# Interleaving a head's gate projection with the next head's query projection

## The chip, the cores and the metric

The kernel runs on one core of a Trainium2 chip. The metric is the device time of one execution in microseconds. A core has a matrix engine (PE, with its weight loads listed as PEld), a vector engine (DVE), an activation engine (ACT), a general engine (POOL) and a queue engine that starts transfers (SP). Each engine works through its own list of instructions in order, and waits on semaphores for the others.

## What is computed

Two layers over 1024 latent tokens of width 1024, with 256 context tokens. The first layer is attention with 16 query heads and 4 key/value heads of width 128, the second a convolution module. The time here is about the first layer; its heads are, cut to what matters:

```python
proj = h_lat @ w_in
q = apply_rope(split_heads(proj[..., :q_end], N_Q_HEADS), cos, sin)
k = apply_rope(split_heads(proj[..., q_end:k_end], N_KV_HEADS), cos, sin)
v = split_heads(proj[..., k_end:v_end], N_KV_HEADS)
z = proj[..., v_end:]
...
o = windowed_attention(q, k, v, kc, vc, sink)
y = (o * jax.nn.silu(z)) @ w_out
```

A query sees the latent keys within 128 positions of it and all context keys. `z` is the gate: one column block of 128 for each head, as for `q`.

## The kernel before

All data are fp32. Each product is made of three matmuls on fp32r parts (high by high, high by low, low by high), so a weight chunk of 1024 x 128 is loaded (`wraw`), copied to its high part on ACT (`whi`) and reduced to its low part on POOL (`wlo`) before PE can use it. `WStream` does this in the order of a list of chunks: z of head n, q of head n + 1, and after every fourth head k and v of the next group.

In the attention stage each head has 8 steps, one for each block of 128 queries. A step issues, in this order on PE: the scores of the next block (`scores`, 6 matmuls into a `pss` bank), a share of projection work (`fill`, usually 12 matmuls into a `psg` bank), from time to time the product with the values (`pv`, into `pso`), and the transposes of the current block's probabilities (`transposes`, into the other kind of `pss` bank). Between scores and transposes DVE takes the maximum with the mask, ACT the exponential, and POOL divides by the sum (`p_page`). After the transposes ACT copies the high part (`pthi`) and DVE the low part (`ptlo`); until both are done the bank can't take the scores of the step after next.

`fill` draws matmuls from a queue of generators, 24 matmuls for each half of 512 tokens. When a half is done, `finish` issues its evaluation: for z a tanh on ACT (`zs_page<-psg`) and a product on DVE; for q and k the rotation (`rope`): a copy on ACT, two transfers that swap the halves of the partitions, a product with the cosine on DVE, a product with the sine and a sum on POOL, a high copy on ACT and a low part on POOL (`ql_page` or `kl_page`). It takes three of six small buffers (`half`).

Two other streams run beside this. `low_parts` splits the output weights: each step it may load a page (`low_page`), take a high copy on ACT (`lhi_half`), subtract on POOL, or write the result back (`wolA`, `wolC`). `ada_rest` multiplies modulation weights on DVE (`mask_page<-dww_raw` or `wsum_raw`).

After heads 3, 7 and 11 the loop regroups: it runs the k and v projections of the next group with no steps between. Between heads, the next head's queries must be enqueued ahead of its first scores:

```python
        if nxt and nxt[1] == 0:
            fill(1000, ("q", h + 1))
        if nxt and not regroup:
            scores(*nxt)
```

PE keeps the order of the program text. On DVE, ACT, POOL and SP a scheduler decides the order when the program is built. Pages of 4 KB per partition come from a first-in first-out list (`Pages`), so the order of frees decides which tile a load must wait for. All instructions are recorded at line 89, in a helper, so groups are told apart by tile names.

Of the kernel before, what the change touches and what calls it, by code (L numbers as in the profile page):

```python
# [19 lines left out]
NH = 16  # L20
# [74 lines left out]
def backbone_kernel(  # L95
# [23 lines left out]
    def nm(s):  # L119
        uid[0] += 1  # L120
        return f"{s}_{uid[0]}"
# [12 lines left out]
    def ps_g():  # L134
        return ps.tile([P, 512], F32, tag="g", name=nm("psg"), bufs=2)
# [13 lines left out]
    def act(out, in_, func, **kw):  # L149
        return A.activation(out=out, in_=in_, func=func, **kw)  # L150
# [4 lines left out]
    def stt(out, in0, scalar, in1, op0, op1):  # L155
        return V.scalar_tensor_tensor(out=out, in0=in0, scalar=scalar, in1=in1, op0=op0, op1=op1)

    def split_lo(eng, lo, full, hi):
        return tt(eng, lo, full, hi.bitcast(F32), ALU.subtract)
# [99 lines left out]
    cidx = {}  # L259
# [14 lines left out]
    wsA = WStream(chunks, nraw=4, lo_eng=lambda i: V if i < 4 else G)  # L274
# [545 lines left out]
    def gemm_half(wc, half, o):  # L820
        wh, wl = wc
        sl = slice(half * 512, half * 512 + 512)
        for kt in range(KT):
            PE.matmul(o, wh[:, kt], Hh[kt][:, sl], start=kt == 0, stop=False)
            yield
            PE.matmul(o, wh[:, kt], Hl[kt][:, sl], start=False, stop=False)
            yield
            PE.matmul(o, wl[:, kt], Hh[kt][:, sl], start=False, stop=kt == KT - 1)
            yield
# [38 lines left out]
    def finish(kind, n, half, o, d, ropes=None, hold=None):  # L868

        sl = slice(half * 512, half * 512 + 512)  # L870
        if kind in "kv" and half == 2:
            c = kvt[n][2]
            if kind == "k":
                act(c[:, 0], o[:, 0:CT], AF.Copy)
                i = split_lo(V, c[:, 1], o[:, 0:CT], c[:, 0])
                while hold:
                    hold.pop()(i)
                return None
        if kind in "qk":
            return rope(o, sl, d[0][:, sl], d[1][:, sl], ropes, hold)  # L880
        if kind == "z":
            act(d[:, sl], o, AF.Tanh, scale=0.5)
            stt(d[:, sl], d[:, sl], 1.0, o, ALU.add, ALU.mult)
            return None
        w = CT if half == 2 else 512
        f = hp.alloc(F32, None, "vf")
        act(f[:, 0:w], o[:, 0:w], AF.Copy)

        def tail():
            if half == 2:  # L890
                vt_split(f, CT, *(c[:, i].rearrange("p (a b) -> p a b", b=P) for i in (2, 3)))
            else:
                vt_split(f, 512, *(t[:, half * 4:half * 4 + 4] for t in d))
            hp.free(f)

        return tail

    def target(kind, n):

        if kind == "q":  # L900
            qt[n] = d = (pg.alloc(F32R, [1024], "qh"), pg.alloc(F32R, [1024], "ql"))
        elif kind == "k":
            kvt[n] = [pg.alloc(F32R, [1024], "kh"), pg.alloc(F32R, [1024], "kl"), pg.alloc(F32R, [4, CT], "kvc")]
            d = kvt[n][0:2]
        elif kind == "v":
            kvt[n] += [pg.alloc(F32R, [TB, P], "vh"), pg.alloc(F32R, [TB, P], "vl")]
            d = kvt[n][3:5]
        else:
            zt[n] = d = pg.alloc(F32, [1024], "zs")
        return d  # L910
# [10 lines left out]
    def job(key):  # L921
        kind, n = key
        i = cidx[key]
        wc = wsA.need(i)
        d = target(kind, n)
        wsA.load()
        late = None
        hold = [] if kind == "k" else None
        for half in PARTS[kind]:
            o = ps_g()  # L930
            gh = gemm_ctx(wc, o) if half == 2 else gemm_half(wc, half, o)
            for m, _ in enumerate(gh):
                yield
                if m == DEFER - 1 and late:
                    late()
            if half == PARTS[kind][0] and wsA.ns <= i + 1:
                wsA.split()
                wsA.load()
            late = finish(kind, n, half, o, d, hold=hold)
        if late:  # L940
            vlate[n] = late
        wsA.done(i)
        if key == ("v", NG - 1):
            for t in Hc:
                pg.free(*t)

    def run(gen):
        for _ in gen:
            pass

    fillq = deque()
    finished = set()

    def fill(n, until=None):
        while n > 0 and fillq and until not in finished:
            try:
                next(fillq[0][1])
                n -= 1
            except StopIteration:
                finished.add(fillq.popleft()[0])  # L960

    def enqueue(key):
        fillq.append((key, job(key)))

    ptile = {}

# [55 lines left out]
    def pv(h, half):  # L1022
        g = h // 4
        c, vh, vl = kvt[g][2:5]
        o = ps_o()
        q0 = half * 4
        work = [(*(c[:, n, i * P:i * P + P] for n in (2, 3)), slice(13 + 4 * i, 17 + 4 * i), slice(0, 512)) for i in range(2)]
        for kb in range(max(q0 - 1, 0), min(q0 + 4, TB - 1) + 1):
            qa, qz = max(kb - 1, q0), min(kb + 1, q0 + 3)
            b0 = 1 + 4 * (1 - (kb - qa)) + (qa - q0)  # L1030
            n = qz - qa + 1
            if n == 1 and kb > qa:
                work.append((vh[:, kb], vl[:, kb], slice(0, 5, 4), slice(256, 512)))
            elif n == 1:
                work.append((vh[:, kb], vl[:, kb], slice(9, 22, 12), slice(0, 256)))
            else:
                work.append((vh[:, kb], vl[:, kb], slice(b0, b0 + 5 * (n - 1) + 1, 5),
                             slice((qa - q0) * P, (qz - q0 + 1) * P)))
        for n, (a, b, ps_, os_) in enumerate(work):
            last = n == len(work) - 1  # L1040
            PE.matmul(o[:, os_], a, pthi[:, ps_], start=n == 0, stop=False)
            PE.matmul(o[:, os_], a, ptlo[:, ps_], start=False, stop=False)
            PE.matmul(o[:, os_], b, pthi[:, ps_], start=False, stop=last)
        sl = slice(half * 512, half * 512 + 512)
        oz = hp.alloc(F32, None, "oz")
        stt(oz[:, 0:512], o, 0.5, zt[h][:, sl], ALU.mult, ALU.mult)
        SY.dma_start(out=ozd[h, :, sl], in_=oz[:, 0:512])
        hp.free(oz)
        if half:
            pg.free(zt.pop(h))  # L1050
            pg.free(*qt.pop(h))
# [49 lines left out]
    lows = low_parts()  # L1101
    lstate = ["shut"]
    pvq = deque()
    enqueue(("z", 0))
    enqueue(("q", 1))
    fill(18)
    while tails:
        tails.pop()()
# [2 lines left out]
    for i, (h, qb) in enumerate(steps):  # L1111
        if qb == 0:
            for n in (() if h % 4 == 3 else (h + 1,) if h % 4 or not h else (h, h + 1)):
                enqueue(("z", n))
                if n + 1 < NH:
                    enqueue(("q", n + 1))
        if (h, qb) == (NH - 1, EARLY_FROM - 2):
            run(lows)
        if h == NH - 1 and EARLY_FROM - 2 <= qb < EARLY_FROM:
            next(projA)  # L1120
        if (h, qb) == (NH - 1, EARLY_FROM):
            next(projA)
            fillq.append((("wo", 0), early_proj()))
        if lstate[0] == "open" or h and (h % 4 < 3 or qb < LOWS):
            lstate[0] = next(lows, "shut")
        nxt = steps[i + 1] if i + 1 < len(steps) else None
        regroup = nxt and nxt[1] == 0 and nxt[0] % 4 == 0
        if nxt and nxt[1] == 0:
            fill(1000, ("q", h + 1))
        if nxt and not regroup:  # L1130
            scores(*nxt)
        if not regroup:
            fill(15 if h and h % 4 == 0 and qb < 4 else FILL)
        if pvq:
            pv(*pvq.popleft())
        if regroup:
            g = nxt[0] // 4
            old = kvt[g - 1]
            run(job(("k", g)))
            transposes(h, qb)  # L1140
            run(job(("v", g)))
            pv(h, 1)
            pg.free(*old)
            scores(*nxt)
            vlate.pop(g)()
            continue
        transposes(h, qb)
        if qb % 4 == 3:
            pvq.append((h, qb // 4))
        for _ in range(2 if qb == 1 or qb == 6 and h % 2 else 1):  # L1150
            next(adag, None)
# [72 lines left out]
    dq, pq = deque(), deque()  # L1224
# [502 lines left out]
```

## Time and profile before

| what | value |
| --- | --- |
| median of 3 runs | 1756.32 us (1753.38 to 1756.82) |
| the profiled execution, its time | 1754.72 us |
| its span, first to last instruction | 1752.9 us |
| mean granted TensorE clock | 0.996 |
| PE busy | 1720.7 us, 98% of the span |
| attention stage, about 100 to 860 us | PE busy 753.28 of 760 us |

A row names an engine, an operation, and the tiles that it writes and reads. A wait in brackets is the time that the engine stood idle ahead of the instruction, and what ended it. In the chain of work that ended last, "issue" is time in which nothing in the profile was waited for.

### The profile page before, as it was taken

The numbers are of one execution on the slowest core, as the hardware profiler recorded it, in microseconds if no ns is written. First come the engines' busy times: TensorE is split into PE (matmuls) and PEld (weight loads), VectorE is DVE, ScalarE is ACT, GpSimd is POOL, SyncE is SP. The second block draws the span as 40 slices with busy tenths as digits, with TensorE's granted clock in tenths as the row PEclk, the third lists the DMA queues.
The fourth block names the chain that finished last, engine by engine and source line by source line (L and its number), as shares of the span: only waits on it lengthen the run. The fifth ranks groups of instructions, "written<-read, shape, count | busy, mean of one in ns | idle before, by whom it ended". The sixth has DMA issues, their size and how long they took to land.

```text
span 1752.9 us, 23877 instructions
## 1 busy us (share of the span) xinstructions
PE 1720.7 (98%) x8420; PEld 1424.8 (81%) x8420; DVE 1148.3 (66%) x2079; ACT 889.4 (51%) x1548; POOL 895.4 (51%) x705
## 2 busy tenths in 40 slices
PE   7999999999999999999999999999999999999997
PEld 4788888888888888888888888888888888788886
DVE  6755564556546563656315189999999999867823
ACT  7555553445345444545334355554665564466731
POOL 0245654566636565653101267998898888130300
PEclk9999999999999999999999999999999999999999
DMA  9334443444334542436777733011121202377971
GB/s 313 107 82 139 136 133 85 145 147 145 100 105 143 152 142 87 136 119 203 279 250 239 241 90 105 13 54 31 43 79 36 91 30 79 120 254 243 325 264 48
DMA packets 195324, 242.45 MB, mean 138 GB/s; under 512 B 11798, under 2 KB 126790, under 8 KB 195204
## 3 DMA queue, kind: packets, MB, share of 16 engines
q1 hardware_dynamic: 188516, 230.10, 40.3%
q10 hardware_dynamic: 6688, 10.83, 2.6%
q8 instruction: 66, 1.08, 0.3%
q14 instruction: 54, 0.44, 0.1%
HBM read 188.70 MB, written 41.69 MB: 131 GB/s over the span
## 4 chain that ended last, share of the span: by engine, by line
PE 86%; DMA 5%; DVE 3%; POOL 2%; ACT 2%; issue 2%; SPq 1%; ACTq 0%; POOLq 0%; DVEq 0%
PE psg L89 44%; PE pss L89 22%; PE pso L89 19%; DMA araw_page<-in_ada_w_dram 1%; POOL rope_half L89 1%; DMA low_page<-in_conv_w_out_dram 1%; DMA rope_half<-rope_half 1%; SPq L89 1%; DMA low_page<-in_attn_w_out_dram 1%; DMA wolC<-low_page 1%; DVE mask_page L89 1%; ACT p_page L89 0%; POOL wlo_page L89 0%; POOL low_page L89 0%; DMA wraw_page<-in_attn_w_in_dram 0%
## 5 line engine op out<-in xcount | busy, mean ns | idle before, releaser
L89 POOL TENSOR_TENSOR odd_half<-odd_half,prod_half 128x513 f32<-128x513 f32 (+2 forms) x252 | 312.8, 1250 | 24.2 <-ACT prod_half L89 11.0
L89 PE MATMUL psg<-hh_page,whi_page 128*128 128x512 f32 x600 | 237.6, 396 | 0.0
L89 PE MATMUL psg<-hh_page,wlo_page 128*128 128x512 f32 x600 | 236.9, 395 | 0.0
L89 PE MATMUL psg<-hl_page,whi_page 128*128 128x512 f32 x600 | 236.8, 395 | 0.0
L89 POOL TENSOR_TENSOR wlo_page<-wraw_page,whi_page 128x1024 fp32r<-128x1024 f32 x70 | 173.1, 2475 | 104.1 <-ACT whi_page L89 83.2
L89 ACT ACTIVATE prod_half<-ubuf,dww 128x513 f32<-128x513 f32 (+2 forms) x252 | 165.1, 674 | 107.3 <-POOL odd_half L89 105.1
L89 POOL TENSOR_SCALAR p_page<-p_page,sc 128x640 f32<-128x640 f32 (+1 forms) x128 | 100.8, 787 | 224.4 <-DVE sc L89 208.7
L89 PE MATMUL psg<-h2h_page,whi_page 128*128 128x512 f32 x464 | 183.9, 396 | 0.0
L89 PE MATMUL psg<-h2h_page,wlo_page 128*128 128x512 f32 x464 | 183.0, 394 | 0.0
L89 PE MATMUL psg<-h2l_page,whi_page 128*128 128x512 f32 x464 | 182.4, 393 | 0.0
L89 DVE SCALAR_TENSOR_TENSOR pss<-ubuf,dww,pss 128x512 f32<-128x512 f32 (+3 forms) x270 | 172.3, 670 | 0.1
L89 DVE SCALAR_TENSOR_TENSOR pss<-ubuf,wsum,pss 128x512 f32<-128x512 f32 (+3 forms) x270 | 171.7, 670 | 0.2
L89 DVE TENSOR_TENSOR ptlo<-pss,pthi 128x640 fp32r<-128x640 f32 (+1 forms) x144 | 103.3, 717 | 64.0 <-ACT pthi L89 62.8
L89 ACT ACTIVATE p_page<-p_page,sc 128x641 f32<-128x641 f32 (+1 forms) x128 | 102.7, 802 | 74.1 <-DVE sc L89 69.7
L89 ACT ACTIVATE pthi<-pss 128x640 fp32r<-128x640 f32 (+1 forms) x144 | 88.6, 615 | 91.7 <-PE pss L89 86.3
L89 PEld LDWEIGHTS psg<-hh_page,wlo_page 128*128 128x128 f32 x600 | 112.9, 188 | 26.3
L89 PEld LDWEIGHTS psg<-hh_page,whi_page 128*128 128x128 f32 x600 | 113.0, 188 | 20.8 <-DVE kvc_page L89 0.2
L89 PEld LDWEIGHTS psg<-hl_page,whi_page 128*128 128x128 f32 x600 | 112.9, 188 | 20.7
L89 ACT ACTIVATE whi_page<-wraw_page 128x1024 fp32r<-128x1024 f32 x88 | 92.6, 1053 | 69.0 <-PE psg L89 25.5
L89 PE MATMUL pso<-h2l_page,whi_page 128*128 128x512 f32 x304 | 119.9, 394 | 0.0
L89 PE MATMUL pso<-h2h_page,whi_page 128*128 128x512 f32 x304 | 119.8, 394 | 0.0
L89 PE MATMUL pso<-h2h_page,wlo_page 128*128 128x512 f32 x304 | 119.6, 394 | 0.0
(244 smaller groups left out, 4105.2 us busy)
## 6 DMA issues: line engine op xcount, KB each, us to landing
wraw_page<-in_conv_w_in_dram SPq DMA_DIRECT2D x48, 512.0 KB
wraw_page<-in_attn_w_in_dram SPq DMA_DIRECT2D x40, 512.0 KB
wol_page<-wolA SPq DMA_DIRECT2D x32, 512.0 KB
wo_page<-in_attn_w_out_dram SPq DMA_DIRECT2D x32, 512.0 KB
wo_page<-in_conv_w_out_dram SPq DMA_DIRECT2D x32, 512.0 KB
wol_page<-wolC SPq DMA_DIRECT2D x32, 512.0 KB
rope_half<-rope_half ACTq DMA_DIRECT2D x80, 128.0 KB
araw_page<-in_ada_w_dram SPq DMA_DIRECT2D x32, 256.0 KB
```

The lines of the kernel that those rows point to most:

```text
L89: r = f(*a, **k)
```

## The change

The two jobs of a head, z of head n and q of head n + 1, become one generator. It makes z for the first 512 tokens, then q for both halves, then z for the second 512. The z weights are held until the end; the q chunk is split when the first half of z is done, and the chunk behind it at the start of the second half of z. Ahead of a `pv` the loop now makes sure that the half of the gate that it needs has been enqueued, and ahead of a regroup that the whole pair has.

```diff
--- before.py
+++ after.py
@@ -944,6 +944,38 @@
             for t in Hc:
                 pg.free(*t)
 
+    def job_pair(n):
+
+        i = cidx[("z", n)]
+        wz = wsA.need(i)
+        dz = target("z", n)
+        wsA.load()
+        o = ps_g()
+        yield from gemm_half(wz, 0, o)
+        if n + 1 < NH and wsA.ns <= i + 1:
+            wsA.split()
+            wsA.load()
+        finish("z", n, 0, o, dz)
+        finished.add(("z0", n))
+        if n + 1 < NH:
+            wq = wsA.need(i + 1)
+            dq = target("q", n + 1)
+            wsA.load()
+            for half in range(2):
+                o = ps_g()
+                yield from gemm_half(wq, half, o)
+                finish("q", n + 1, half, o, dq)
+            wsA.done(i + 1)
+            finished.add(("q", n + 1))
+        o = ps_g()
+        for m, _ in enumerate(gemm_half(wz, 1, o)):
+            yield
+            if m == 0 and n + 1 < NH and wsA.ns <= i + 2:
+                wsA.split()
+                wsA.load()
+        finish("z", n, 1, o, dz)
+        wsA.done(i)
+
     def run(gen):
         for _ in gen:
             pass
@@ -959,8 +991,8 @@
             except StopIteration:
                 finished.add(fillq.popleft()[0])
 
-    def enqueue(key):
-        fillq.append((key, job(key)))
+    def enqueue(n):
+        fillq.append((("z", n), job_pair(n)))
 
     ptile = {}
 
@@ -1101,8 +1133,7 @@
     lows = low_parts()
     lstate = ["shut"]
     pvq = deque()
-    enqueue(("z", 0))
-    enqueue(("q", 1))
+    enqueue(0)
     fill(18)
     while tails:
         tails.pop()()
@@ -1111,9 +1142,7 @@
     for i, (h, qb) in enumerate(steps):
         if qb == 0:
             for n in (() if h % 4 == 3 else (h + 1,) if h % 4 or not h else (h, h + 1)):
-                enqueue(("z", n))
-                if n + 1 < NH:
-                    enqueue(("q", n + 1))
+                enqueue(n)
         if (h, qb) == (NH - 1, EARLY_FROM - 2):
             run(lows)
         if h == NH - 1 and EARLY_FROM - 2 <= qb < EARLY_FROM:
@@ -1126,12 +1155,13 @@
         nxt = steps[i + 1] if i + 1 < len(steps) else None
         regroup = nxt and nxt[1] == 0 and nxt[0] % 4 == 0
         if nxt and nxt[1] == 0:
-            fill(1000, ("q", h + 1))
+            fill(1000, ("z", h) if regroup else ("q", h + 1))
         if nxt and not regroup:
             scores(*nxt)
         if not regroup:
             fill(15 if h and h % 4 == 0 and qb < 4 else FILL)
         if pvq:
+            fill(1000, ("z" if pvq[0][1] else "z0", pvq[0][0]))
             pv(*pvq.popleft())
         if regroup:
             g = nxt[0] // 4
```

The order of the instructions shows it at three places. The first is on PE in head 1, where the first half of the gate ends. `psg` is the accumulator, `hh` and `hl` are the input's parts, `whi` and `wlo` the weights'. Before:

```order
L89 MATMUL psg_1365<-hh_page_643,whi_page_1240 128x512
L89 MATMUL psg_1365<-hl_page_644,whi_page_1240 128x512
L89 MATMUL psg_1365<-hh_page_643,wlo_page_1241 128x512
L89 MATMUL psg_1453<-hh_page_310,whi_page_1240 128x512
L89 MATMUL psg_1453<-hl_page_311,whi_page_1240 128x512
L89 MATMUL psg_1453<-hh_page_310,wlo_page_1241 128x512
L89 MATMUL psg_1453<-hh_page_316,whi_page_1240 128x512
L89 MATMUL psg_1453<-hl_page_317,whi_page_1240 128x512
```

And now:

```order
L89 MATMUL psg_1365<-hh_page_643,whi_page_1262 128x512
L89 MATMUL psg_1365<-hl_page_644,whi_page_1262 128x512
L89 MATMUL psg_1365<-hh_page_643,wlo_page_1263 128x512
L89 MATMUL psg_1455<-hh_page_310,whi_page_1445 128x512
L89 MATMUL psg_1455<-hl_page_311,whi_page_1445 128x512
L89 MATMUL psg_1455<-hh_page_310,wlo_page_1446 128x512
L89 MATMUL psg_1455<-hh_page_316,whi_page_1445 128x512
L89 MATMUL psg_1455<-hl_page_317,whi_page_1445 128x512
```

The accumulator that follows took the same weight pages before (the second half of the gate) and takes the next chunk's now (the queries), so that chunk must be split 24 matmuls sooner.

The second is on POOL ahead of the first regroup. Before, from the low part of the k weights on:

```order
L89 TENSOR_TENSOR wlo_page_2643<-wraw_page_2277,whi_page_2642 128x1024
L89 TENSOR_SCALAR p_page_2578<-p_page_2578,sc_2579 128x512
L89 TENSOR_TENSOR wlo_page_2947<-wraw_page_2646,whi_page_2946 128x1024
L89 TENSOR_TENSOR rope_half_2592<-rope_half_2592,sin_page_664 128x512
L89 TENSOR_TENSOR rope_half_2593<-rope_half_2593,rope_half_2592 128x512
L89 TENSOR_TENSOR rope_half_2649<-rope_half_2649,sin_page_664 128x512
L89 TENSOR_TENSOR ql_page_2391<-rope_half_2593,qh_page_2390 128x512
L89 TENSOR_TENSOR kl_page_2615<-rope_half_2650,kh_page_2614 128x512
```

And now:

```order
L89 TENSOR_TENSOR wlo_page_2643<-wraw_page_2277,whi_page_2642 128x1024
L89 TENSOR_SCALAR p_page_2587<-p_page_2587,sc_2588 128x512
L89 TENSOR_TENSOR wlo_page_2947<-wraw_page_2646,whi_page_2946 128x1024
L89 TENSOR_TENSOR rope_half_2649<-rope_half_2649,sin_page_664 128x512
L89 TENSOR_TENSOR kl_page_2615<-rope_half_2650,kh_page_2614 128x512
L89 TENSOR_TENSOR rope_half_2682<-rope_half_2682,sin_page_664 128x512
```

The first rotation (2592, 2593, with its `ql_page`) was that of the second half of the queries of head 4 and stood among the two rotations of k (2649, 2650); now it is gone from there, since these queries were rotated earlier.

The third is on ACT and SP in head 9 to 10, around a load of `low_page`. Before, on ACT and then on SP:

```order
L89 ACTIVATE pthi<-pss_5610 128x2x128 x2
L89 ACTIVATE p_page_5632,sc_5633<-p_page_5632,sc_5633 128x641
L89 ACTIVATE lhi_half_5708<-low_page_5672 128x512
L89 ACTIVATE lhi_half_5758<-low_page_5672 128x512
L89 ACTIVATE pthi<-pss_5660 128x5x128
L89 ACTIVATE p_page_5681,sc_5682<-p_page_5681,sc_5682 128x641
L89 ACTIVATE whi_page_5839<-wraw_page_5428 128x1024
L89 ACTIVATE zs_page_5533<-psg_5647 128x512
```

```order
L89 DMA wolC<-low_page_5506 128x1024
L89 DMA ozd<-oz_half_5607 128x512
L89 DMA low_page_5672<-in_conv_w_out_dram 128x2x512
L89 DMA wsum_raw<-in_ada_w_dram 128x256
L89 DMA low_page_5823<-in_conv_w_out_dram 128x2x512
```

And now, where the same weight rows are loaded (page 5674), ACT and SP:

```order
L89 ACTIVATE pthi<-pss_5463 128x5x128
L89 ACTIVATE p_page_5484,sc_5485<-p_page_5484,sc_5485 128x513
L89 ACTIVATE whi_page_5639<-wraw_page_5227 128x1024
L89 ACTIVATE lhi_half_5710<-low_page_5674 128x512
L89 ACTIVATE zs_page_5118<-psg_5444 128x512
L89 ACTIVATE pthi<-pss_5503 128x5x128
```

```order
L89 DMA wraw_page_5450<-in_attn_w_in_dram 128x8x128
L89 DMA ozd<-oz_half_5397 128x512
L89 DMA dww_raw<-in_ada_w_dram 128x256
L89 DMA low_page_5674<-in_conv_w_out_dram 128x2x512
L89 DMA wolC<-low_page_5347 128x1024
```

On ACT two copies of the loaded page stood right ahead of `pthi`; now one does, with a weight split ahead of it. On SP the load followed a write (`wolC`) that waits for POOL; now that write comes behind it, and the load's page is the one that the low part of a head's queries has just left.

## Rows read from the trace of the kernel before

**Rows 1.** The page's line of busy times and their shares of the span.

```profile
PE 1720.7 (98%) x8420; PEld 1424.8 (81%) x8420; DVE 1148.3 (66%) x2079; ACT 889.4 (51%) x1548; POOL 895.4 (51%) x705
```

**Rows 2.** Stages: window, its length, then busy us of each engine, clock, DMA share.

```profile
100.00:860.00 760.00, 753.28 (x4151) 649.60 (x4150) 423.52 (x832) 368.21 (x774) 410.91 (x347) 1.00 0.44 136
860.00:1490.00 630.00, 630.00 (x2766) 512.42 (x2765) 496.64 (x820) 327.40 (x471) 426.64 (x312) 1.00 0.32 103
```

**Rows 3.** Waits of PE from 100 to 860 us: total, times, longest.

```profile
PE pss L89 <- DVE ptlo L89: 3.6, 2, 3.2
PE pss L89 <- DVE sc L89: 1.3, 3, 0.9
...
PE psg L89 <- DVE rope_half L89: 1.0, 1, 1.0
PE pss L89 <- POOL p_page L89: 0.5, 1, 0.5
```

**Rows 4.** POOL in order of time ahead of the first regroup's wait.

```profile
268.88 2.41 POOL L89 TENSOR_TENSOR wlo_page<-wraw_page,whi_page 128x1024 fp32r<-128x1024 f32 x1 [4.37 <-ACT whi_page L89]
271.25 1.48 POOL L89 TENSOR_TENSOR rope_half<-rope_half,sin_page 128x512 f32<-128x512 f32 x1
272.80 1.29 POOL L89 TENSOR_TENSOR rope_half<-rope_half,rope_half 128x512 f32<-128x512 f32 x1
274.06 1.30 POOL L89 TENSOR_TENSOR rope_half<-rope_half,sin_page 128x512 f32<-128x512 f32 x1
275.30 1.31 POOL L89 TENSOR_TENSOR ql_page<-rope_half,qh_page 128x512 fp32r<-128x512 f32 x1
```

**Rows 5.** DVE in order of time at the same place.

```profile
276.65 0.69 DVE L89 TENSOR_TENSOR rope_half<-psg,cos_page 128x512 f32<-128x512 f32 x1 [4.48 <-POOL ql_page L89]
```

**Rows 6.** The chain that ended last, 560 to 600 us: start, us, what.

```profile
571.22 4.17 DMA rope_half<-rope_half
...
578.26 1.29 POOL rope_half L89
...
582.46 6.16 DMA low_page<-in_conv_w_out_dram
...
588.64 1.15 ACT lhi_half L89 x2
589.79 0.60 ACT pthi L89
...
590.41 0.84 DVE ptlo L89
...
591.29 1.15 PE pss L89 x6
592.43 2.78 PE psg L89 x12
595.22 0.55 PE pss L89 x5
...
596.10 1.00 PE pss L89 x6
```

**Rows 7.** The same chain, 343 to 354 us.

```profile
343.89 4.87 DMA low_page<-in_attn_w_out_dram
...
351.64 1.27 DVE mask_page L89
352.91 0.80 DVE p_page L89
```

**Rows 8.** POOL, then ACT, where head 1's first gate half ends.

```profile
140.32 2.41 POOL L89 TENSOR_TENSOR wlo_page<-wraw_page,whi_page 128x1024 fp32r<-128x1024 f32 x1
...
146.77 0.60 ACT L89 ACTIVATE zs_page<-psg 128x512 f32<-128x512 f32 x1 [0.53 <-PE psg L89]
```

**Rows 9.** A load of `low_page` on SP, and the copy on ACT that waits for it.

```profile
412.41 0.38 SPq L89 DMA_DIRECT2D low_page<-in_attn_w_out_dram  x1
...
416.46 0.63 ACT L89 ACTIVATE lhi_half<-low_page 128x512 fp32r<-128x512 f32 x1 [1.62 <-DMA low_page<-in_attn_w_out_dram]
```

## Prediction

> **What bounds the kernel now.** I began with the page's busy times. PE is busy for 98% of the span [rows 1], so a change of order can only win PE's idle time or add to it. Then I cut the span into stages: the changed loop runs from about 100 to 860 us, and there PE is busy for 753.28 of 760 us, at a granted clock of 1.00 [rows 2]. So at most 6.7 us can be won in that stage. The stage behind it (860 to 1490 us) has no idle time on PE at all [rows 2], so what is won or lost ahead of it should arrive at the end undiminished.
>
> Third, the waits of PE in the stage: 3.6 us for `ptlo` on DVE (two waits, one of 3.2), 1.3 us for `sc` on DVE (three waits), 1.0 us for DVE's part of a rotation, and 0.5 us for `p_page` on POOL [rows 3]. That is 6.4 us. No row among them is a wait of scores for the queries' low part or of `pv` for the gate. The change therefore can't pay by making queries ready "in time": they are. It can pay only through what else moves on ACT, POOL and SP.
>
> Last, the chain through the larger waits. The 3.2 us wait is not DVE's doing: a rotation's transfer took 4.17 us, POOL began that rotation's sum 7 us after the transfer's start, the queue issued the next `low_page` load only at 582.46, this load took 6.16 us, and `pthi` stood behind the two copies of that page on ACT [rows 6]. The waits for `sc` look alike: the longest hangs on a `low_page` load of 4.87 us, followed by a modulation product that took 1.27 us and the scores' maximum on DVE [rows 7]. The 1.0 us wait at the first regroup has another form: POOL stood still for 4.37 us, then had a low part of 2.41 us, and then worked off the rotations of the last queries and of k one by one [rows 4]; DVE's product, which empties PE's bank, waited until the queries' `ql_page` had given back its buffers [rows 5].
>
> **The change part by part.** The number of instructions and of bytes is the same: each head has the same 96 projection matmuls, two rotations, two gate halves and the same weight splits. What differs is when each engine gets them.
>
> *The rotations come 24 matmuls (one half) earlier.* At the first regroup the rotation of the second query half is gone from POOL's list: a sum of 1.29 us, a `ql_page` of 1.31 us, and a product with the sine of 1.48 us [rows 4]. These are 4.1 us of POOL's work ahead of DVE's product, which was 1.0 us late [rows 3]. I count this wait as removed: −1.0 us. If only the buffers' order mattered and they are still late, it stays: bounds −1.0 and 0.
>
> *The streams beside it shift.* In the order now, the load of `low_page` at the place of the 3.2 us wait comes ahead of the write that waits for POOL, and only one copy of it stands ahead of `pthi`, where there were two. A rotation's transfer and POOL's sums no longer stand between it and its issue. The other `ptlo` wait (0.4 us) is the same place four heads earlier. Both go: −3.6 us, bounds −3.6 and 0. For the waits for `sc`, the load that caused the longest now stands about 12 us of PE work ahead of its copy, where it stood 8 us ahead (matmuls between them in the order, 0.23 us each by 12 in 2.78 us [rows 6]); I count 1.0 of the 1.3 us as removed, since one of the three places keeps its order: bounds −1.3 and 0. The 0.5 us wait for `p_page` is behind the third regroup, where POOL's list still has a rotation, a low part of queries and a weight's low part ahead of the division; it stays.
>
> *New tight places.* The load that now comes earlier (page 5674, and its like four heads before) waits for a group of scores to leave its page. From there PE does 12 matmuls in 2.78 us and 5 transposes in 0.55, then scores in 1.00, 12 matmuls and transposes again [rows 6], until it wants the bank back: 7.66 us. Of these ACT needs one copy (1.15 for two, so 0.6), the gate's tanh, 0.60 [rows 8], and `pthi`, 0.60; DVE needs 0.84 for `ptlo` [rows 6]; the issue takes 0.38 [rows 9]. That leaves 4.6 us for the load. The rows have loads of this size at 6.16 [rows 6], 4.87 [rows 7], and, from issue to the copy, 4.05 us [rows 9]. The wait would be 1.6, 0.3 or 0 us; I take 0.6, the mean, at two places: +1.2 us, bounds 0 and 3.2. At two more places (the load of rows 9 and its like) both copies now stand ahead of `pthi`, where one did. It landed after 4.05 us with no wait of PE; another 0.6 us of copy may cost nothing or 0.6: +0.4 for both, bounds 0 and 1.2.
>
> The Trainium skill (DMA: Bandwidth & Descriptors, Anatomy of one DMA) fits a transfer issued by GpSimd with 2.0 us plus bytes at 436 GB/s, which gives an estimate of 3.2 us for 512 KB; these loads are issued by SP. By that page both kinds of place would be free and the sum 1.6 us lower; the trace doesn't agree with it here, where the loads share the queues with others and took 4.05 to 6.16 us.
>
> *Weights are needed earlier.* The query chunk is split at the end of the first gate half in the text, and its first matmul follows at once. What hides this is that the scheduler has put the split far ahead: in head 1 the low part of that chunk ran at 140.32 for 2.41 us, so it was done at 142.73, and the gate half ended where its tanh began, at 146.77 [rows 8]. The order on POOL around it is nearly the same now, so 4.0 us of slack are left where there were some 20. I count 0. If that cover were gone, PE would wait for as long as POOL is late beyond 4.0 us.
>
> *The gate's second half comes later*, but its reader (`pv` of the second half) is issued in the next head's first step, some 10 us of PE work after its last matmul; tanh 0.60 [rows 8] and a product fit into that. 0 us. The weights of the gate stay in pages for 48 matmuls longer, so that pages go round faster; the loads that this delays are those priced above.
>
> **Sum.** −1.0 −3.6 −1.0 +1.2 +0.4 = −4.0 us. The profiled execution took 1754.7 us, so 1750.7. It lies 1.6 us below the median of the runs shown and 0.6 below the mean of those runs and itself (1755.3). I forecast for runs like that mean: 1751.3 us.
>
> **The rivals.**
>
> *The gaps move and fill up again (no change that can be told).* For it: the waits removed come from loads of 4.87 to 6.16 us on a shared queue [rows 6, 7], and the new places leave only 4.6 us; slow loads there cost 3.2 and 1.2 us, the upper bounds, and if the waits for `sc` stay too, the sum is −1.0 −3.6 +4.4 = −0.2 us: 1755.1 us. Half of that is as likely, 1753.2. Against it: the largest wait needed three delays in a row, a slow rotation, POOL's backlog and the slowest load.
>
> *All loads land as fast as the quick one.* With 4.05 us [rows 9] no new place costs anything: −5.6 us, 1749.7 us. This is also the outcome that the page's 3.2 us stands for. Against it: two of the three loads whose rows are shown were slower than the 4.6 us that are left.
>
> *The weights come too late (slower).* In five heads (0, 1, 2, 4 and 8) the query chunk's low part has only 4 to 6 us of slack. Ahead of it on ACT and POOL stand copies of loaded pages and rotations. If one of them waits for a load of 6.16 us [rows 6] with nothing to spare, PE starts the queries 2.2 us late; five times that is +11 us, which turns −4.0 into +7.0: 1762.3 us. It decides from the point where POOL's low part ends more than 4.0 us later than it did. Against it: at the place shown, POOL went from `p_page` straight to the low part [rows 8], and the rotation that follows it there is one that the change takes away.
>
> *The change does nothing*, since no row shows PE waiting for queries: then the time stays at 1755.3 us. The first rival covers it in time and chance.
>
> **How the numbers follow.** Forecast 0.42 (its own range 1749.8 to 1753), quick loads 0.13, gaps refilled 0.33, weights late 0.12. A difference under 0.2% (3.5 us) can hardly be told from none here. The forecast is 4.0 us better, just beyond that line, so I give most of it, 0.36, to faster; with the quick loads 0.49. Slower by as much needs the late weights in at least four heads: 0.10. The rest, 0.41, is no change that can be told. The range that holds 8 in 10 reaches from the quick loads with their spread to the refilled gaps with the runs' own spread: 1748 to 1757.
>
> **What would show it.** Right: PE's wait for DVE's rotation at the first regroup is gone; the longest wait for `ptlo` in the stage is under 2 us; PE is busy for 4 us more of the same 760 us; the matmuls on the query chunk never wait for `wlo`. Wrong: a new wait of PE for `wlo` or `whi` at the start of a query half, a wait of scores for `ptlo` over 3 us, or waits of the same total at other places. The prediction fails altogether if PE waits as little as said and the time doesn't follow, since then the stages behind would bound the end.

## The result and the profile after

The change made the kernel slower: 1761.37 us (median of 7 runs, 1758.58 to 1763.75) against 1756.04 us (7 runs, 1753.38 to 1758.04), a ratio of 1.0031 with a 95% interval of 1.0019 to 1.0044. The profiled execution took 1761.37 us with a span of 1759.6 us.

The waits of PE from 100 to 860 us, and the stages, of the changed kernel (columns as in [rows 2, 3]):

```profile
PE pss L89 <- DVE ptlo L89: 4.8, 2, 2.4
PE pss L89 <- DVE sc L89: 1.8, 3, 0.9
PE pss L89 <- POOL hl_page L89: 1.2, 1, 1.2
PE pss L89 <- POOL p_page L89: 0.5, 1, 0.5
```

```profile
100.00:860.00 760.00, 751.98 (x4129) 646.85 (x4130) 415.80 (x830) 367.99 (x775) 410.92 (x340) 1.00 0.43 135
860.00:1497.00 637.00, 637.00 (x2796) 517.03 (x2795) 499.24 (x825) 328.43 (x472) 427.92 (x320) 1.00 0.32 103
```

The wait of 1.0 us for `rope_half` [rows 3] is gone, and so are both old waits for `ptlo`. But there are two new ones of 2.4 us each, and the waits for `sc` are longer by half a microsecond. (The row for `hl_page` is a wait of the setup that ends at 100.44 us; the same wait of 1.2 us ended at 99.50 before, ahead of the window.) PE is busy for 751.98 us where it was 753.28 [rows 2], of which 0.4 us are that wait, and the next stage again has no idle time in which this could be made good.

The two new waits are alike and stand 197 us apart, at the starts of heads 5 and 9. The chain through the first, in order of time (start, us, what):

```profile
323.76 1.24 POOL low_page L89
325.00 0.83 POOL rope_half L89
325.83 5.25 DMA wolA<-low_page
331.08 0.02 issue
331.09 3.94 DMA low_page<-in_attn_w_out_dram
335.04 0.02 issue
335.06 0.04 ACT lhi_half L89
...
335.60 0.61 ACT lhi_half L89
336.21 0.09 ACT p_page L89
336.31 0.49 ACT zs_page L89
336.79 0.94 ACT whi_page L89
...
338.15 0.70 ACT pthi L89
...
338.88 0.83 DVE ptlo L89
...
339.76 1.14 PE pss L89 x6
```

Read it from the end: scores wait for `ptlo`, `ptlo` for `pthi`, and `pthi` stands on ACT behind two copies (`lhi`), the gate's tanh (`zs`) and a weight split (`whi`). The copies wait for a load of `low_page`, and this load waits for a *write*. The queue SP says the same (what it waited for, in total, times, longest, from 324 to 336 us):

```profile
SPq L89 <- PE pss L89: 4.9, 2, 3.5
SPq L89 <- DMA wolA<-low_page: 4.8, 1, 4.8
```

The write reads the page into which the load goes. The pool hands out pages first in, first out. Following its list through the program shows why: as the gate's weights are kept for longer, four pages stay free when the `low_page` just ahead takes its page, where six did, so that pages come round sooner, and the next load's turn falls on the page that this `low_page` has just given back. That happens in two of 32 loads, the tenth and the twentieth, which are these two. In the old order no load got such a page.

A second loss hangs on the first wait (windows of PE: window, length, busy us and count of PE, PEld, DVE, ACT, POOL, then the granted clock), shown with three matmuls of that stretch:

```profile
339.70:341.40 1.70, 1.64 (x9) 1.55 (x10) 1.70 (x2) 1.37 (x3) 1.70 (x1) 0.97 0.00 0
341.40:344.80 3.40, 3.40 (x9) 2.62 (x9) 3.34 (x7) 0.92 (x2) 2.54 (x3) 0.51 0.34 92
344.80:350.00 5.20, 5.20 (x34) 4.84 (x34) 1.77 (x3) 1.08 (x3) 0.81 (x1) 1.00 0.55 199
```

```profile
341.96 0.63 PE L89 MATMUL psg<-hl_page,whi_page 128*128 128x512 f32 x1
342.39 0.63 PE L89 MATMUL psg<-hh_page,wlo_page 128*128 128x512 f32 x1
342.81 0.63 PE L89 MATMUL psg<-hh_page,whi_page 128*128 128x512 f32 x1
```

For 3.4 us the clock is half (1.2 instead of 2.4 GHz). Seven matmuls follow each other after 0.43 us instead of 0.23, so 1.4 us are lost in which PE counts as busy.

PE issues matmuls of the same shapes in the same order in both kernels, so each can be set against its twin. The matmul that waits for `hl_page` comes at 100.44 us (99.50 before), the transposes that wait for `p_page` behind the third regroup at 726.81 (722.62 before): 3.3 us between them. Before, the waits in this stretch add up to 5.9 us, now to 6.7; with the 1.4 us of the clock that is 2.2 of the 3.3. Another 0.6 us come at 423.17 and 618.53 us, where scores wait for `ptlo` for 0.10 and 0.06 us, too little for the table, and PE falls back by 0.3 us against its twin each time. The remaining half a microsecond lies in still smaller steps, which I can't assign. (A row of the table understates a wait a little: the first matmul behind each of the two waits of 2.4 us falls back by 2.65 us.)

The 0.9 us at the start are no effect of the change: in the profiles of kernels with the new order alone, below, that matmul comes between 97.9 and 100.4 us. From 726.81 to 1504.05 us another 0.9 us gather in small steps. The last 1.6 us are a wait at 1626.91 us, behind a load of 7.35 us in the last stage. At the same place the other kernels below that have the new order in most heads wait for 0.2 to 1.8 us, with or without the reused page, and those with the old order for 0 to 0.3; each is one execution, so a part of the change in it is not shown. Together this makes up the 6.65 us between the two profiled executions; the medians differ by 5.3.

### The profile page after: what moved, and what is told of

Its sections match the earlier page's. It is cut to its first block, busy times and chain, and to the rows that moved or that the text cites. A ratio compares the mean times of both kernels' runs of the same rounds, so it can differ in the third digit from the quotient of the medians.

```text
span 1759.6 us, 23864 instructions
## 1 busy us (share of the span) xinstructions
PE 1724.6 (98%) x8420; PEld 1425.1 (81%) x8420; DVE 1141.2 (65%) x2079; ACT 889.8 (51%) x1548; POOL 896.1 (51%) x705
## 4 chain that ended last, share of the span: by engine, by line
PE 88%; DMA 5%; DVE 2%; ACT 2%; POOL 1%; issue 1%; SPq 1%; ACTq 0%; DVEq 0%; POOLq 0%
PE psg L89 46%; PE pss L89 23%; PE pso L89 20%; DMA araw_page<-in_ada_w_dram 1%; SPq L89 1%; DMA wolC<-low_page 1%; DMA x_page<-in_x_dram 0%; DMA low_page<-in_attn_w_out_dram 0%; DMA low_page<-in_conv_w_out_dram 0%; DMA wo_page<-in_conv_w_out_dram 0%; DMA rope_half<-rope_half 0%; DMA wraw_page<-in_attn_w_in_dram 0%; DVE mask_page L89 0%; DMA wolA<-low_page 0%; ACT whi_page L89 0%
```

## The experiments

**Away with the page (three ways).** First, a rule in the pool:

```diff
-        i = self.free_.popleft()
+        i = next((j for j in self.free_ if name != "low" or self.last.get(j) != "low"), self.free_[0])
+        self.free_.remove(i)
```

> The changed kernel, with one rule in the page pool: a low_page load takes the first free page whose last user was not a low_page. Two loads change their page (the tenth and the twentieth of the stream, at the starts of heads 5 and 9); PE's program is the same, row for row. Theory (page reuse: the gate's weights stay longer, four pages are free instead of six, so these two loads get the page that the write just ahead of them still reads): both waits of scores for ptlo of 2.4 us go, and the half-speed stretch behind the first one (7 matmuls at 0.43 instead of 0.23 us, 1.4 us): 1761.4 - 2 x 2.4 - 1.4 = 1755.2 us. Rival (the new order on ACT, with copies, a split and qh ahead of pthi, is late whenever the load starts): waits over 1 us stay at both places, 1759 to 1761 us. Rival (the 5 us come from the stages ahead and behind, 0.9 us by 100 us and 1.3 us in the last stage): no less than 1759 us.

Measured: 1754.96 us, ratio to before 0.9994 (0.9985 to 1.0002); the theory gave 1755.2. The waits for `ptlo` shrank to one of 0.2 us, and there is no stretch at half clock in the stage. ACT's order changed near these two loads too, since the copies now move ahead, so this run alone doesn't tell page and order apart. That the time is so close to the theory's is in part luck, since the waits for `sc` grew by 2.5 us (L92 and L97 below are the same helper, in kernels where it stands at another line):

```profile
PE pss L92 <- DVE sc L92: 4.3, 6, 1.1
...
PE pss L92 <- DVE ptlo L92: 0.2, 1, 0.2
```

One of these waits, of 0.99 us at 335.67 us, hangs on the same write, which is as slow as before though no load waits for it any more. In the chain it now holds up a modulation product on DVE:

```profile
327.08 5.83 DMA wolA<-low_page
...
333.56 1.39 DVE mask_page L92
334.95 0.66 DVE p_page L92
```

Second, the old order of projections in the two heads behind which it happens:

```diff
     def enqueue(n):
-        fillq.append((("z", n), job_pair(n)))
+        if n not in (4, 8):
+            fillq.append((("z", n), job_pair(n)))
+            return
+        for key in [("z", n)] + ([("q", n + 1)] if n + 1 < NH else []):
+            fillq.append((key, job(key)))
```

> The changed kernel, with the old order (gate whole, then queries) in heads 4 and 8 alone, and the new order in the other heads. The two loads then get pages that no write reads. Theory (page reuse, which arises only behind heads 4 and 8): both waits of 2.4 us and the half-speed stretch go, and the gain at the regroup of head 4 and of head 8 stays as it comes from heads 3 and 7: 1755 us, at most 1756.5. Rival (splitting the gate costs something in every head): a sixth of the loss goes, 1760.5 us.

Measured: 1753.69 us, ratio 0.9990 (0.9980 to 0.9999). Both waits are gone and the regroup's gain stays. The rival, a cost of the split gate in every head, would have been 1760.5 us and is out. Third, the load of the next weights a step later, which keeps one more page free:

```diff
             if m == 0 and n + 1 < NH and wsA.ns <= i + 2:
                 wsA.split()
-                wsA.load()
+            if m == 12 and n + 1 < NH:
+                wsA.load()
```

> The changed kernel, with the load of the next weights 12 matmuls later in the second gate half (behind its split, not at once). No low_page load gets the page of the low_page just ahead of it any more. Theory (page reuse behind a late write): as with the page rule, 1754.5 to 1756 us, no wait for ptlo over 0.5 us at the starts of heads 5 and 9. Rival (weights come too late when loaded later): waits of PE for whi or wlo, over 1757 us.

Measured: 1755.58 us, ratio 0.9994 (0.9985 to 1.0002); no wait of PE for `whi` or `wlo`, and the largest for `ptlo` is 0.5 us. Three ways to avoid the page take back 6 to 8 us each.

**The page in the old order (two ways).** If the reused page were enough, it should hurt in the old order too.

```diff
-        i = self.free_.popleft()
+        i = self.free_[0]
+        if name == "low":
+            if self.nlow in (9, 19):
+                i = next(j for j in reversed(self.free_) if self.last.get(j) == "low")
+            self.nlow += 1
+        self.free_.remove(i)
```

> The kernel before, with the tenth and the twentieth low_page load made to take the page that the low_page just ahead of them gave back; order of projections as before, PE's program the same. Theory (page reuse): the two loads wait for the write of their page (5.3 to 5.8 us in the changed kernel), land some 5 us later, and pthi behind their copies is late: two new waits of scores for ptlo of 1.5 to 3 us, 1756.0 + 3 to 6 = 1759 to 1762 us. Rival (the order on ACT of the changed kernel is what costs): no new wait over 0.5 us, 1755.5 to 1757 us.

Measured: 1757.02 us, ratio 1.0007 (0.9997 to 1.0016). My theory had said 3 to 6 us more, and it failed here: there is no wait for `ptlo` near 335 us and one of 0.2 near 535, though the load does wait for the write. The queue, in order of time:

```profile
323.00 0.33 SPq L97 DMA_DIRECT2D wolA<-low_page  x1
324.67 0.33 SPq L97 DMA_DIRECT2D ozd<-oz_half  x1
325.92 0.38 SPq L97 DMA_DIRECT2D low_page<-in_attn_w_out_dram  x1
```

The write was issued at 323.00 instead of 325.83 us and was done within 2.9 us instead of 5.25. So the load started 5.2 us earlier than in the changed kernel, and the copies waited for 0.2 us. A reused page therefore costs nothing by itself; it costs when the load behind it comes too late. Then the weights were held longer, without any change of order:

```diff
-        wsA.done(i)
+        if kind != "z" or n + 1 == NH:
+            wsA.done(i)
+        if kind == "q":
+            wsA.done(i - 1)
```

> The kernel before, order of projections unchanged, but the pages of the gate's weights are given back only when the next queries' chunk is done, so that they are held at least as long as in the changed kernel (24 matmuls longer than there). Four low_page loads of the stream get the page of the low_page just ahead (the 6th, 10th, 16th, 20th). Theory (page reuse): two to four new waits of scores for ptlo of 1 to 3 us each, 1759 to 1766 us. Rival (the order of projections costs): within 1 us of the kernel before, 1755 to 1757 us.

Measured: 1759.40 us, ratio 1.0022 (1.0012 to 1.0032). PE waited seven times for `ptlo`, 6.2 us in all, in the stage. So the longer hold alone, at the old order of the matmuls, costs as much as the theory's lower end. But it doesn't confirm the theory's way there. Of the four loads that it names only the tenth waited for its page's write on SP, for 1.3 us. Two of the seven waits (at 148.6 and 190.5 us) come ahead of the first of these loads, and in the 10 us ahead of each wait the chain runs over a write of a `low_page` at one alone, of 0.61 us at 380.9 us. The longest, 1.74 us at 814.3 us, hangs on another load (`ozf_page<-ozd`), of 7.16 us, and the clock is half behind it. Holding the weights longer costs in more ways than the reused page.

**What makes the write slow.** In the changed kernel three transfers of 512, 256 and 512 KB are issued within 1.1 us (SP, in order of time):

```profile
324.77 0.38 SPq L89 DMA_DIRECT2D wraw_page<-in_attn_w_in_dram  x1
325.25 0.53 SPq L89 DMA_DIRECT2D ozd<-oz_half  x1
325.83 0.42 SPq L89 DMA_DIRECT2D wolA<-low_page  x1
331.09 0.38 SPq L89 DMA_DIRECT2D low_page<-in_attn_w_out_dram  x1
```

The next two runs force the reuse into the kernel of the later load, where it had vanished; the second also puts the weights' load behind the write:

```diff
-            SY.dma_start(out=r, in_=self.srcs[i].rearrange("(k p) n -> p k n", p=P))
+            d = SY.dma_start(out=r, in_=self.srcs[i].rearrange("(k p) n -> p k n", p=P))
+            if behind:
+                after(d, anchor_w)
```

> The kernel of the later next load (which cost 1755.6 us and had no reuse), with the tenth and the twentieth low_page load again made to take the page that the low_page just ahead of them gave back. On the queue the load of the next weights still stands ahead of that page's write. Theory (the reuse costs when the write is late and slow): write of over 5 us, load landing 9 us after the write's issue, waits for ptlo of 1.5 to 2.5 us at both places, 1758.5 to 1761 us. Rival (reuse is harmless when the rest is shifted a little): below 0.7 us each, 1756 us.

> As the run before, but the load of the next weights stands behind the write on the queue at the two places. Theory (the write is slow, 5.3 to 5.8 us, since it shares the queues with the weights' load issued 1 us ahead of it; in the old order with the reuse forced the load of the page started 2.9 us after the write): the write takes 3 to 3.5 us, the low_page load lands 2 us or more earlier, waits for ptlo under 0.6 us each, 1755 to 1757 us. Rival (the write is late for POOL's sake and the queue doesn't matter): waits as in the run before, 1758.5 to 1761 us.

Measured: 1755.31 us, ratio 0.9994 (0.9985 to 1.0003), with the load ahead, and 1756.33, ratio 0.9999 (0.9991 to 1.0008), with it behind. The first expectation failed: no wait at either place. The weights' load had come 3.7 us ahead of the write (319.38 and 323.11 us), not 1.1, and the page's load started 2.65 us after the write. In the second run, with the weights' load 0.9 us behind the write, the chain was:

```profile
325.75 2.68 DMA wolA<-low_page
...
328.50 6.99 DMA low_page<-in_attn_w_out_dram
...
335.51 1.15 ACT lhi_half L97 x2
```

The write is quick now and the load slow. From the write's issue to the load's end it takes 9.7 us, as in the changed kernel (9.2). PE waited for 1.1 us at this place and not at all at the other. So the second expectation got the time, but not its reason: the load landed no earlier, and the wait was not under 0.6 us. At this place it isn't the order of the two on the queue that counts: 9.2 and 9.7 us with the weights' load within 1.1 us of the write on either side, 6.6 us to the copies with 3.7 us between them. That issuing them together is what makes it slow is suggested by this, but not shown. At the other place the same two runs take 8.1 us with 3.4 us between the two and 8.9 us with the weights' load 1.5 us behind the write, and PE waits at neither; and in the kernel of the next section the page's load still waits 4.4 us for its write with the weights' load issued 2.6 us ahead.

The Trainium skill (DMA: Bandwidth & Descriptors, Anatomy of one DMA) fits a GpSimd-issued transfer in a way that gives an estimate of 3.2 us for 512 KB. The transfers here are issued by SP: the write with no 512 KB issued close ahead of it is near that, at 2.7 us; the two with one ahead, at 5.25 and 6.99, are not.

**Copies behind `pthi`.** The other half of the chain is ACT's order. Each copy of a `low_page` was ordered behind the newest `pthi`:

```diff
-                act(hi[:, 0:512], raw[:, b], AF.Copy)
+                after(act(hi[:, 0:512], raw[:, b], AF.Copy), anchor_t)
...
-            act(pthi[:, bs], tv[:, r0:r1], AF.Copy)
+            anchor_t[:] = [act(pthi[:, bs], tv[:, r0:r1], AF.Copy)]
```

> The changed kernel, with each copy of a low_page (lhi) ordered behind the newest pthi on ACT; the two loads still get the page that a write reads, PE's program is the same. Theory as it stands after the first four runs (the loss needs both: a load that waits for its page's write, and copies of it ahead of pthi on ACT): both waits for ptlo of 2.4 us and the half-speed stretch go, about 1755 us. Rival (a late load costs what it costs, wherever the copies stand, since POOL and SP behind it are late too): waits of together over 3 us at these places or a step later, 1759 to 1762 us.

Measured: 1755.35 us, ratio 0.9995 (0.9986 to 1.0004). The reuse is still there, and the queue still waits 4.4 and 4.0 us for the two writes, but the waits of 2.4 us for `ptlo` are down to 0.12 and 0.11 us. So at these two places the loss needs both: a late load, and copies of it ahead of `pthi`. The kernel is no faster than before for it, since PE now waits for 2.9 us for `sc` and 2.8 us for `p_page`. The same edit in the kernel before:

> The kernel before, with each copy of a low_page (lhi) ordered behind the newest pthi on ACT. Theory (copies that wait for a load hold up pthi): the waits for ptlo of 3.2 and 0.4 us go, 1756.0 - 3.6 = 1752.4 us. Rival (the low parts then come later, so that writes, loads and the modulation's loads on the same queue are late): as much is lost at waits for sc or ptlo, 1755 to 1758 us.

Measured: 1749.96 us (5 runs, 1749.20 to 1750.96), ratio 0.9960 (0.9946 to 0.9973). This is the lowest median of all versions, 0.4% below the kernel before. Its waits of PE, 100 to 860 us:

```profile
PE pss L89 <- POOL p_page L89: 1.4, 2, 0.7
...
PE psg L89 <- DVE rope_half L89: 1.0, 1, 1.0
PE pso L89 <- DVE ptlo L89: 0.7, 1, 0.7
PE pss L89 <- DVE sc L89: 0.5, 1, 0.5
```

The old waits for `ptlo` are gone, as the theory said, and those for `sc` fell from 1.3 to 0.5 us, which it hadn't counted. The rows of the stage fell from 6.4 to 3.6 us and the profiled executions differ by 3.8 us (1754.72 and 1750.96). The medians of that comparison differ by 6.8 us; what makes up the rest is not shown.

Three combinations ask whether the new order can gain on top of that: this edit with that of the two heads, with the page rule, and with the new order in heads 3, 7 and 11 alone.

> The new order except in heads 4 and 8, and each copy of a low_page behind the newest pthi on ACT. Theory: of the 2.9 us of waits that this mixed order has left, only one of 0.2 us is for ptlo, so 0 to 0.3 us better than the mixed order alone: 1753.5 us. Rival (later copies make new waits): 1755 us or more.

> The changed kernel with both cures: no low_page load takes the page of the low_page just ahead of it, and each copy of a low_page stands behind the newest pthi on ACT. Theory (the new order also makes POOL and DVE late elsewhere: with the copies behind pthi alone it had waits of 2.8 us for p_page and 2.9 for sc, where the old order with the same cure had 1.4 and 0.5): 1754 to 1756 us, so 4 to 6 us above the old order with its cure. Rival (those waits too come from the late page): at the old order's level or 1 us better, as the wait at the first regroup is gone, 1749 to 1751 us.

> The new order in heads 3, 7 and 11 alone (those whose next queries are rotated ahead of a regroup), the old order in the others, and each copy of a low_page behind the newest pthi on ACT; no load gets the page of the low_page just ahead in the stretch of heads 4 to 10. Theory (the regroup term of the prediction is right by itself): the wait of 1.0 us for the rotation at the first regroup goes, the rest is as in the old order with the same cure (1750.0 us): 1749 us. Rival (the new order just ahead of a regroup makes POOL late behind it, as with both cures, where PE waited 2.7 us for p_page behind the third): 1751 to 1753 us.

Measured: 1753.96 us, ratio 0.9985 (0.9976 to 0.9994); 1754.75 us, ratio 0.9993 (0.9983 to 1.0003); 1752.37 us, ratio 0.9976 (0.9967 to 0.9985). The first two came as their theories said (1753.5 us, and 1754 to 1756). The third theory, 1749 us, failed: the time is its rival's. No median reaches that of the old order with its cure, though the interval of the third, 0.9967 to 0.9985, overlaps with that one's, 0.9946 to 0.9973. With both cures PE waits for 3.2 us for `sc` and for 2.7 us for `p_page`:

```profile
709.88 4.71 DMA rope_half<-rope_half
...
714.72 1.30 POOL rope_half L92
716.03 0.07 issue
716.09 1.28 POOL rope_half L92
717.38 1.24 POOL low_page L92
718.62 0.49 POOL ql_page L92
...
719.82 2.36 POOL wlo_page L92
722.18 0.96 POOL p_page L92
```

In this chain behind the third regroup POOL does a rotation, a low part, `ql` and a weight's low part before the division (`p_page`) that PE needs; in the old order with its cure POOL has the same list there, but the rotation's transfer took 2.37 us instead of 4.71, and the wait was 0.7. So this wait hangs on one slow transfer, and that the new order causes it is not shown. The run with the new order ahead of the regroups alone shows the term that was right, by itself: the wait for `rope_half` is gone, but waits for `sc` went from 0.5 to 2.5 us, where its rival had expected them for `p_page`.

## Why the prediction was wrong

**Right.** PE had no wait for queries or the gate, so only what moves on the other engines counted. The regroup's wait (-1.0 us) went. Both old waits for `ptlo` (-3.6) went. The weights were never late: no wait of PE for `whi` or `wlo` (0), so that rival is out; that its time, 1762.3 us, lies near the measured one is chance. The gate's second half cost nothing, and the `p_page` wait stayed at 0.5. A loss did arrive at the end undiminished, as the stage behind has no idle time.

**Wrong: the step on the pages.** "The weights of the gate stay in pages for 48 matmuls longer, so that pages go round faster; the loads that this delays are those priced above." The loads that it delayed were two others. I had followed which page a load gets only at the place whose old wait vanished, and had taken a free page to be ready when the load is issued. At the starts of heads 5 and 9 the page was still being written out: 4.8 us for two waits, and 1.4 us of half clock, in place of 0. Together, 6.2 us, they outweigh the 4.6 that was won. That these two places are the loss is shown by the runs that take away the reused page or move the copies: each is 5.8 to 7.7 us below the changed kernel.

**Wrong: the price of the new tight places.** The +1.2 us (the load of page 5674 and its like) measured nothing: no wait for `ptlo` remains there. The load took 4.0 us to the copy that waited for it, inside the 4.6 us that I had left for it, where I had taken the mean of three waits, two of them from slower loads (SP, then ACT):

```profile
570.62 0.38 SPq L89 DMA_DIRECT2D low_page<-in_conv_w_out_dram  x1
...
574.66 0.63 ACT L89 ACTIVATE lhi_half<-low_page 128x512 fp32r<-128x512 f32 x1 [0.43 <-DMA low_page<-in_conv_w_out_dram]
```

The +0.4 us (the load of [rows 9] and its like) came about right: both copies do stand ahead of `pthi` there, and these are the two places, at 423.17 and 618.53 us, where PE falls back by 0.3 us each.

**Wrong: the waits for `sc`.** I counted -1.0 of 1.3 us; they are 1.8 us. The old places went and new ones came; the chains through two of the three (at 227 and 570 us) run over a modulation product on DVE that started late. In the run with the page rule they are 4.3 us, which is the largest row that keeps that version level with the kernel before. The other repaired versions have 1.8 to 3.2 us of them.

**The rival that came nearest** is the first, gaps that refill, in kind: waits of much the same total at other places. Its price was too low, as it knew neither these places nor the clock. The limit that I had set as a sign of failure in `ptlo`, 3 us, was not reached by one wait; the sum of the two and the fall of the clock did it. The range, to 1757, had no room for a wait outside the places that I had looked at.

## What to carry to other kernels

When a change holds buffers for longer, follow each buffer of the pool from its last reader to its next writer; where the last reader is a write to memory, the next load waits for it, and in a queue that works in order so does all behind it. In these runs a reused page cost only where the load came late and something that PE needs stood behind its copies: look at both ends, and order the copies of prefetched data behind the work that is waited for. This kernel, which waits for 6 us in 760, gained little from a better order of one stream, since as many microseconds turned up in another; the largest gain, 0.4%, came from taking a whole kind of dependence away.

## What the hardware showed unexpectedly

The clock fell to half for 3.4 us behind one idle time of 2.40 us of PE, but not behind the other of 2.42 (the clock stays 1.00 there), nor behind 3.19 us in the kernel before [rows 3]. With both cures it fell at the wait of 2.7 us (0.57 over 722.5 to 726.5 us), with the copies behind `pthi` alone it stayed at 1.00 behind one of 2.62 us at the same matmul, and with the weights held longer it fell behind one of only 1.74 us (0.55 over 814.6 to 818.4 us). So in these runs the length of the wait doesn't decide. What does was not tried; that a wait can cost half as much again is what a sum has to allow for.
